# Norms of token blocks in one VectorE operation, a shared tile for the halves' last rows, and steps of two blocks in turn

## The chip, the cores and the metric

The kernel runs on one core of a Trainium2 chip. The engines are TensorE (PE in the profile, its weight loads PEld), VectorE (DVE), ScalarE (ACT), GpSimd (POOL) and SyncE (SP, which here only issues DMAs). Each engine takes its instructions in a fixed order and waits on semaphores. The metric is the device time of one execution in microseconds (us); lower is better.

## The reference

Two layers of a decoder run over 1040 prompt rows (16 learned rows and 1024 tokens) and 32 sample rows of width 1024. The change touches the first layer, a gated convolution; the attention layer behind it (`mla_query`, `attend`) stays as it is.

```python
def conv_mixer(h, prev, w_in, conv_w, w_out):
    L = h.shape[1]
    b_gate, c_gate, u, z = jnp.split(h @ w_in, 4, axis=-1)
    v = c_gate * u
    vc = jnp.concatenate([prev.astype(v.dtype), v], axis=1)
    y = conv_w[0] * vc[:, 0:L]
    for k in range(1, CONV_WIDTH):
        y = y + conv_w[k] * vc[:, k:k + L]
    out = (b_gate * y * jax.nn.silu(z)) @ w_out
    return out, vc[:, L:]
...
h = rmsnorm(x, pre_norm_g[l])
m, st = conv_mixer(h, conv_prev[l], w_in_conv[l], conv_w[l], w_out_conv[l])
x = x + rmsnorm(m, post_norm_g[l])
```

## The kernel before

All 1072 rows are treated as one matrix. Float32 operands are split into a high part (`hi_of`, an ACT copy with rounding) and a low part (`lo_of`, a subtraction, on DVE unless another engine is named), and a product takes three matmuls: high by high, high by low, low by high. The input product of the convolution is computed by a seven-product scheme for 2x2 blocks: the rows are cut into two halves of HT = 536 (`l` = 0 and 1), the width into two halves of 512. The seven left operands are held turned (features on partitions) in `H`: "11" and "21" are the first row half, "22" the second row half's upper width, "t1" to "t4" sums. The right operands of a pair of weight tiles are made by `weight_sums`: four POOL additions s1 to s4, then a high and a low part for each of seven operands.

**The opening.** Each half is read in five blocks (`PAIRS`): four of 128 rows and one of 24. `loaded` fetches a block, `normed` norms it: ACT squares it with a row sum (`junk`, `ss`), POOL makes the scale (`ta`, `qa`). A first-half block is then multiplied by the gain on POOL (`x<-x,gain`) and scaled on ACT (`x<-x,qa`); a second-half block takes one DVE operation (`x<-x,qa,gain`) and a subtraction `t3`. A block becomes steps in the list `todo`: `turn_in` (four PE transposes into a PSUM bank), for some steps `add_in` (two matmuls that add a finished part with +1 or -1), and `put` (a high part by ACT, a low part by DVE, both read from PSUM). A first-half block has two steps, a second-half block five: `chain` (t3), `plain` (22), `more` (t2), `other` (t1), `more` (t4). The two `more` steps add to the bank that `chain` filled, so each waits until the low part before it has been read. `Pair.start(ch)` computes two products of a unit early from the first half alone, for the columns of `CUTS[ch]` (256, then 280): 12 matmuls, an ACT copy `k1`, 12 more into the same bank, a copy `c11`. `Pair.multiply(n, ch)` is one of the seven products, 12 matmuls; the first unit runs `ORDER` = 1, 6, 5, 7, 3, 2, 4 (1 and 2 are the early ones) for `ch` 0 between the steps, then for `ch` 1. Fifteen more units follow.

**The end of the convolution.** Seven of eight gated rows go through DRAM (`gd`) into `g`, the last is written by four DVE operations (`Row.gate`). Then each pair of output weights is loaded (`raw`, three buffers) and split into `woh` and `wol`; `gated(b)` splits a token block of `g` into `gh` and `gl`, and PE computes `po`. The space of `woh` and `wol` is that of the input weights (`wr`), which is released when the last unit is done (`l2.close()`).

The order on each engine comes from the code's order and `tc.issue_after` (it keeps PE's instructions behind a marked one), through a scheduler that orders instructions by modelled times and gives tiles their slots. `tile(..., tag, bufs)` gives one of `bufs` slots, whose last reader must be done.

## Time and profile before

| | before |
|---|---|
| median of 3 runs | 1384.45 us (1381.78 to 1392.17) |
| profiled execution, its time | 1382.27 us |
| its span, first to last instruction | 1380.2 us |
| PE busy | 1295.8 us (94%) |
| DVE, ACT, POOL busy | 854.0, 680.1, 616.7 us |
| mean granted TensorE clock | 0.970 of full speed |

The span is cut into instructions by engine. A row of the timeline has a start, a length, the engine and line, what it writes and reads, the shape and a count; in brackets stands the idle time before it and the instruction that ended it. Matmuls overlap, so the distance of two starts tells more than a length. A share of busy time is a mean over stages: PE is almost always busy after the opening, so what an engine does beside it costs nothing there.

### The profile page before, as it was taken

What the parts mean: (1) busy time and instruction counts of PE and PEld (TensorE: products, weight loads), DVE (VectorE), ACT (ScalarE), POOL (GpSimd) and SP (SyncE); (2) the same over time, 40 slices, a digit from 0 to 9 for tenths busy, and PEclk for the clock granted to TensorE, in tenths of its full rate; (3) what the DMA queues carried; (4) which work ended last, traced back from release to release, by engine and by line L of the source; (5) the groups of instructions that cost most, each with busy time, mean ns of one, the idle gap of its engine ahead of it and who ended that gap; (6) DMA issues with size and microseconds to landing.
All of it is one profiled execution on the core that took longest, in us unless ns stands there. A gap on an engine that the chain in (4) does not pass through costs nothing.

```text
span 1380.2 us, 22927 instructions
## 1 busy us (share of the span) xinstructions
PE 1295.8 (94%) x8142; PEld 1169.0 (85%) x8142; DVE 854.0 (62%) x1750; ACT 680.1 (49%) x1401; POOL 616.7 (45%) x829
## 2 busy tenths in 40 slices
...
GB/s 173 47 64 52 75 79 50 76 62 48 80 247 92 90 85 106 47 147 208 212 80 1 40 62 25 47 63 25 62 41 32 72 215 176 113 148 129 114 168 169
DMA packets 107149, 131.86 MB, mean 96 GB/s; under 512 B 21135, under 2 KB 80187, under 8 KB 107035
## 3 DMA queue, kind: packets, MB, share of 16 engines
...
q8 instruction: 65, 1.06, 0.3%
...
## 4 chain that ended last, share of the span: by engine, by line
PE 42%; DMA 8%; DVE 5%; ACT 2%; issue 2%; POOL 1%; SPq 1%; DVEq 0%; POOLq 0%; ACTq 0%
PE pa L69 10%; PE ps L69 8%; PE pm L69 6%; PE pz L69 6%; PE pf L69 3%; DMA qh<-qd32h 3%; PE pr L69 3%; PE po L69 2%; DMA cn<-in_cache_ckv_dram,crow 2%; PE pc L1388 1%; PE pt L69 1%; DMA qd32h<-qxh 1%; DMA rr<-rl 1%; DVE big L850 1%; SPq L988 1%
## 5 line engine op out<-in xcount | busy, mean ns | idle before, releaser
L79 DVE TENSOR_TENSOR wl<-raw,wh 128x512 fp32r<-128x512 f32 x88 | 75.1, 857 | 99.3 <-ACT wh L74 95.9
L74 ACT ACTIVATE wh<-raw 128x512 fp32r<-128x512 f32 x88 | 55.1, 630 | 129.7 <-PE pa L69 48.2
L1169 ACT ACTIVATE p<-ps 128x512 f32<-128x512 f32 (+1 forms) x192 | 93.2, 492 | 38.3 <-PE ps L69 33.9
L74 ACT ACTIVATE ph<-p 128x512 fp32r<-128x512 f32 (+1 forms) x192 | 97.3, 527 | 22.1 <-POOL p L1174 20.7
L69 PE MATMUL pz<-ph,v 128*128 128x512 f32 (+3 forms) x384 | 104.8, 360 | 0.4 <-ACT ph L74 0.2
L79 POOL TENSOR_TENSOR nl<-cn,nh 128x256 fp32r<-128x256 f32 x64 | 62.0, 987 | 90.6 <-ACT nh L74 81.9
L79 POOL TENSOR_TENSOR pl<-p,ph 128x512 fp32r<-128x512 f32 (+2 forms) x75 | 82.5, 1109 | 32.7 <-ACT ph L74 26.1
L79 DVE TENSOR_TENSOR pl<-p,ph 128x512 fp32r<-128x512 f32 (+3 forms) x117 | 79.3, 684 | 26.7 <-ACT ph L74 26.2
L1025 DVE TENSOR_REDUCE mx<-pm 128x1 f32<-128x16 f32 (+6 forms) x210 | 83.6, 423 | 16.9 <-PE pm L69 16.4
L1174 POOL TENSOR_SCALAR_AFFINE_SELECT p<-p 128x127 f32<-128x127 f32 (+1 forms) x128 | 47.0, 370 | 81.2 <-ACT p L1169 61.6
L69 PEld LDWEIGHTS pz<-ph,v 128*128 128x128 f32 x384 | 66.3, 193 | 7.3 <-ACT ph L74 1.2
L69 PE MATMUL pm<-kh,qh 128*128 128x144 f32 (+6 forms) x210 | 61.6, 343 | 10.6 <-DMA qh<-qd32h 10.4
L69 PE MATMUL ps<-qh,kh 97*128 97x512 f32 (+3 forms) x192 | 68.6, 357 | 1.9 <-DMA qh<-mr 0.9
L69 PE MATMUL pz<-pl,v 128*128 128x512 f32 (+1 forms) x192 | 68.0, 355 | 1.6 <-DVE pl L79 1.2
L69 PE MATMUL ps<-qh,kl 97*128 97x512 f32 (+3 forms) x192 | 67.4, 351 | 0.0
L69 PE MATMUL ps<-ql,kh 97*128 97x512 f32 (+3 forms) x192 | 67.2, 350 | 0.0
L108 POOL TENSOR_SCALAR ta<-ss 128x1 f32<-128x1 f32 (+2 forms) x37 | 8.4, 227 | 126.6 <-ACT xa L605 52.7
L69 PE MATMUL pa<-x1h,wh 128*128 128x352 f32 x288 | 64.1, 329 | 0.0
L69 PE MATMUL pa<-x1h,wl 128*128 128x352 f32 x288 | 63.9, 328 | 0.0
L69 PE MATMUL pa<-x1l,wh 128*128 128x352 f32 x288 | 62.8, 326 | 0.0
L74 ACT ACTIVATE wh<-s 128x512 fp32r<-128x512 f32 x48 | 30.0, 630 | 64.8 <-POOL s L173 26.2
L79 DVE TENSOR_TENSOR wl<-s,wh 128x512 fp32r<-128x512 f32 x48 | 47.3, 989 | 21.3 <-ACT wh L74 20.0
...
## 6 DMA issues: line engine op xcount, KB each, us to landing
...
```

The costliest lines, as they stand in the source:

```text
L69: return pe.matmul(out, a, b, start=start, stop=stop, **kw)
L74: return act.activation(out, src, AF.Copy, scale=scale)
L79: (eng or dve).tensor_tensor(out, src, f(hi), ALU.subtract)
L108: pool.tensor_scalar(t[:r], ss[:r], 1.0 / n, EPS, ALU.mult, ALU.add)
L850: dve.tensor_tensor(qo, qo, sw, ALU.add)
L988: sp.dma_start(f(q[e * DN:e * DN + DN]), f(dn[h * DN:(h + 1) * DN]))
L1025: dve.tensor_reduce(mx[:, b, c:c + 1], pm[:, :off], AX.X, ALU.max)
L1169: act.activation(pt[:r, :n], ps[:r, :n], AF.Exp, scale=SCALE)
L1174: marks[h] = marks.get(h, []) + [pool.affine_select(pt[:r, :dn], pt[:r, :dn], [[1, dn]], ALU.is_ge, 0.0, base=META + c0 - t * P, channel_m ...
L1388: state["turned"] = pe.transpose(pc[:, r], cn[:, r, c * P:(c + 1) * P], ident)
```

## The change

Six edits are made together. (1) A block's gain and scale are one DVE operation for both halves. (2) The 24 last rows of the two halves share one tile: the first half's at partition 0, the second's at 32, 56 partitions in all with a POOL `memset` of the gap; one norm serves both, and this block comes fifth instead of fifth and tenth. (3) x tiles have four slots instead of three, and loads are issued in another order. (4) Steps of two second-half blocks are interleaved, `other` comes before the first `more`, and the early products, the weight sums and the banks (`spaces`) are placed anew. (5) The low parts of the first unit's five further weights are made on POOL (`eng=pool`). (6) `H["11"]` is allocated last in `hp`; the tiles `x1h`, `x1l` of the next stage are allocated first on the right side, and behind them the first two pairs of output weights (`wo2`), in the space of `H["11"]`.

```diff
-        H = {q: [hp.tile([P, HK, HT], F32R, name=f"h{q}{n}") for n in "hl"] for q in ("11", "21", "22", "t3", "t4")}
+        H = {q: [hp.tile([P, HK, HT], F32R, name=f"h{q}{n}") for n in "hl"] for q in ("21", "22", "t3", "t4", "11")}
...
-        def parts_w(src):
+        def parts_w(src, eng=None):
...
-            lo_of(wl, src, wh)
+            lo_of(wl, src, wh, eng)
...
-        def weight_sums(w1, w2, have=()):
+        def weight_sums(w1, w2, have=(), eng=None):
...
-            return {n: parts_w(src) for n, src in zip(ORDER, (a11, s2, s1, s3, s4, a12, a22)) if n not in have}
+            return {n: parts_w(src, eng) for n, src in zip(ORDER, (a11, s2, s1, s3, s4, a12, a22)) if n not in have}
...
         minus = xs.tile([P, P], F32R, name="minus")
         marks = {}
+
+        blocks = [(0, p) for p in range(4)] + [(None, 4)] + [(1, p) for p in range(4)]
+        ROWS = {0: 0, 1: 32}
+
         def loaded(l, p):
             lo, r = PAIRS[p]
-            x = xs.tile([P, D], F32, tag="x", bufs=3, name="x")
-            load_x(x, l * HT + lo, r, sp)
+            x = xs.tile([P, D], F32, tag="x", bufs=4, name="x")
+            if l is None:
+                pool.memset(x[:ROWS[1] + r], 0.0)
+                for l, at in ROWS.items():
+                    load_x(x[at:at + r], l * HT + lo, r, sp)
+            else:
+                load_x(x, l * HT + lo, r, sp)
             return x
         def normed(l, p, x):
-            lo, r = PAIRS[p]
+            r = PAIRS[p][1] if l is not None else ROWS[1] + PAIRS[p][1]
             junk = wr.tile([P, D], BF16, tag="sm", bufs=3, name="junk")
             ss = stat.tile([P, 1], F32, tag="ss", name="ss")
             act.activation(junk[:r], x[:r], AF.Square, accum_out=ss[:r])
             rs = rstd_of(ss, D, r, "a")
+            dve.scalar_tensor_tensor(x[:r], x[:r], rs[:r], gain[:r], ALU.mult, ALU.mult)
             if l == 0:
-                pool.tensor_tensor(x[:r], x[:r], gain[:r], ALU.mult)
-                act.activation(x[:r], x[:r], AF.Copy, scale=rs[:r])
-                return x
-            dve.scalar_tensor_tensor(x[:r], x[:r], rs[:r], gain[:r], ALU.mult, ALU.mult)
+                return first_half(p, x, slice(0, r))
+            rows = slice(0, r) if l else slice(ROWS[1], r)
             t3 = wr.tile([P, 512], F32, tag="sm", bufs=3, name="t3")
-            dve.tensor_tensor(t3[:r], x[:r, :512], x[:r, 512:], ALU.subtract)
-            return x, t3
+            dve.tensor_tensor(t3[rows], x[rows, :512], x[rows, 512:], ALU.subtract)
+            return ([] if l else first_half(p, x, slice(0, PAIRS[p][1]))) + second_half(p, x, t3, rows)
         def put(p, q, pt):
             lo, r = PAIRS[p]
             hi_of(hi, pt[:, :, :r])
             lo_of(lo_, pt[:, :, :r], hi)
-        def turn_in(p, pt, src):
+        def turn_in(p, pt, src, rows):
             r = PAIRS[p][1]
             for k in range(HK):
-                marks["pe"] = pe.matmul(pt[:, k, :r], src[:r, k * P:(k + 1) * P], ident[:r, :r], start=k == 0, stop=k == HK - 1, is_transpose=True, skip_group_check=True).ins
+                marks["pe"] = pe.matmul(pt[:, k, :r], src[rows, k * P:(k + 1) * P], ident[rows, rows], start=k == 0, stop=k == HK - 1, is_transpose=True, skip_group_check=True).ins
         def add_in(p, pt, sign, q):
             tag = spaces.pop(0)
             return four(turned() if tag == "t" else bank(tag))
-        def first_half(p, h):
...
+        def first_half(p, h, rows):
...
+        def second_half(p, h, t3, rows):
...
-                turn_in(p, at[0], t3)
...
-            return [chain, plain, lambda: more("t2", minus, "11"), other, lambda: more("t4", plus, "21")]
+            return [chain, plain, other, lambda: more("t2", minus, "11"), lambda: more("t4", plus, "21")]
...
         keep_warm(turned(), WARM)
         hi_of(plus, ident)
         hi_of(minus, ident, -1.0)
-        blocks = [(l, p) for l in range(2) for p in range(5)]
-        xt = {b: loaded(*b) for b in blocks[:2]}
+        xt = {blocks[0]: loaded(*blocks[0])}
         sp.dma_start(gain, i["pre_norm_g"][0:1].to_broadcast((P, D)))
+        xt[blocks[1]] = loaded(*blocks[1])
+        w0 = conv_w(0)
         xt[blocks[2]] = loaded(*blocks[2])
-        w0 = conv_w(0)
         z0 = conv_w(2)
+        xt[blocks[3]] = loaded(*blocks[3])
         w1 = conv_w(1)
-        todo = []
-
-        def stage(*some):
-            for b in some:
-                h = normed(*b, xt.pop(b))
-                todo.extend(first_half(b[1], h) if b[0] == 0 else second_half(b[1], *h))
-                n = blocks.index(b) + 3
-                if n < len(blocks):
-                    xt[blocks[n]] = loaded(*blocks[n])
-
-        stage(*blocks[:2])
-        a0, a1, b0, b1 = w0[:, :512], w0[:, 512:], z0[:, :512], z0[:, 512:]
-        first = Pair(None, 0, {1: parts_w(a0), 2: parts_w(a1)}, early=True)
-        second = Pair(None, 1, {1: parts_w(b0), 2: parts_w(b1)}, early=True)
-        spaces += ["t", "t", "c0", "c1"] * 8
+
+        def stage(n):
+            res = normed(*blocks[n], xt.pop(blocks[n]))
+            if n + 4 < len(blocks):
+                xt[blocks[n + 4]] = loaded(*blocks[n + 4])
+            return res
+
+        first = Pair(None, 0, {1: parts_w(w0[:, :512]), 2: parts_w(w0[:, 512:])}, early=True)
+        spaces += ["t", "t", "c0", "c1", "a1", "b1"]
+        todo = stage(0) + stage(1)
         steps(todo, 4)
-        stage(*blocks[2:5])
-        for unit in (first, second):
-            for _ in unit.start(0):
-                steps(todo, 2 if len(todo) > 3 else 1)
+        second = Pair(None, 1, {1: parts_w(z0[:, :512]), 2: parts_w(z0[:, 512:])}, early=True)
+        spaces += ["t", "t", "c0", "c1"] * 3
+        todo = stage(2) + stage(3)
+        early = [x for unit in (first, second) for x in (unit.start(0), unit.start(1))]
+        for n in (0, 0, 2, 2):
+            next(early[n])
+            steps(todo, 1)
+        todo += stage(4)
+        first.w.update(weight_sums(w0, w1, have=(1, 2), eng=pool))
+        first.sums()
+        steps(todo, 2)
+        spaces[:] = ["t", "c0", "t", "c1", "a0", "b0"] * 2
+
+        todo2 = [stage(n) for n in (5, 6)]
+        todo += todo2[0][:3] + todo2[1][:1] + todo2[0][3:4] + todo2[1][1:3] + todo2[0][4:] + todo2[1][3:]
+        next(early[1])
+        steps(todo, 3)
+        next(early[1])
+        steps(todo, 4)
+        next(early[3])
+        steps(todo, 4)
+        next(early[3])
         steps(todo, len(todo))
-        first.w.update(weight_sums(w0, w1, have=(1, 2)))
-        first.sums()
-        stage(*blocks[5:7])
-        del spaces[6:]
-        for unit in (first, second):
-            for _ in unit.start(1):
-                steps(todo, 3)
-        spaces += ["t", "c1", "a1", "t", "b1", "a0"] * 4
-
-        stage(*blocks[7:])
+        spaces[:] = ["t", "c1", "t", "a1", "b1", "a0"]
+        todo2 = [stage(n) for n in (7, 8)]
+        todo = todo2[0][:3] + todo2[1][:1] + todo2[0][3:4] + todo2[1][1:3] + todo2[0][4:] + todo2[1][3:]
+
         for n in ORDER:
             if n not in (1, 2):
                 with tc.issue_after(marks["pe"]):
                     first.multiply(n, 0)
-                steps(todo, 3)
+                steps(todo, 3 if n in (6, 5) else 2)
+        steps(todo, len(todo))
...
         l2.close()
         l0.close()
+        x1s = ctx.enter_context(ExitStack())
+        x1p = x1s.enter_context(sbuf("x1p", side="right"))
+        x1h = x1p.tile([P, NK, T], F32R, name="x1h")
+        x1l = x1p.tile([P, NK, T], F32R, name="x1l")
+
+        w2 = l1.enter_context(sbuf("wo2", side="right"))
         wr = l1.enter_context(sbuf("wo"))
...
         wo = []
         for k in range(NK):
             raw = load_w(i["w_out_conv"][0, k * P:(k + 1) * P])
-            wh, wl = (wr.tile([P, D], F32R, name=f"wo{n}{k}") for n in "hl")
+            wh, wl = ((w2 if k < 2 else wr).tile([P, D], F32R, name=f"wo{n}{k}") for n in "hl")
             hi_of(wh, raw)
             lo_of(wl, raw, wh)
             wo.append((wh, wl))
...
-        x1s = ctx.enter_context(ExitStack())
-        x1p = x1s.enter_context(sbuf("x1p", side="right"))
-        x1h = x1p.tile([P, NK, T], F32R, name="x1h")
-        x1l = x1p.tile([P, NK, T], F32R, name="x1l")
```

ACT at the start, before (`junk` is the square, `x<-x,qa` the scaling, `wh` a weight's high part, `pt` and `c` PSUM banks):

```order
L198 ACTIVATE junk,ss<-x 128x1024 x3
L202 ACTIVATE x<-x,qa 128x1024
L74 ACTIVATE wh<-raw 128x512 x4
L202 ACTIVATE x<-x,qa 128x1024
L74 ACTIVATE h11h<-pt 128x4x128
```

ACT at the start, now:

```order
L207 ACTIVATE junk,ss<-x 128x1024 x2
L74 ACTIVATE wh<-raw 128x512 x2
L74 ACTIVATE h11h<-pt 128x4x128
L74 ACTIVATE h21h<-pt 128x4x128
L207 ACTIVATE junk,ss<-x 128x1024
L74 ACTIVATE wh<-raw 128x512
L74 ACTIVATE h11h<-c_204 128x4x128
L74 ACTIVATE wh<-raw 128x512
```

The scalings are gone, and the first block is read from PSUM behind two squares and two weight parts instead of three, four and two scalings.

POOL behind the first squares, before (`s_355` to `s_357` are s1, s2, s4; `raw<-raw` is s3):

```order
L172 TENSOR_TENSOR s_355<-raw 128x512
L108 TENSOR_SCALAR ta<-ss 128x1
L201 TENSOR_TENSOR x<-x,gain 128x1024
L173 TENSOR_TENSOR s_356<-raw,s_355 128x512
L174 TENSOR_TENSOR raw<-raw 128x512
L110 TENSOR_TENSOR qa<-ta,mhalf 128x1
L108 TENSOR_SCALAR ta<-ss 24x1
L201 TENSOR_TENSOR x<-x,gain 24x1024
L175 TENSOR_TENSOR s_357<-raw,s_356 128x512
```

POOL in the same place, now:

```order
L110 TENSOR_TENSOR qa<-ta,mhalf 56x1
L172 TENSOR_TENSOR s_343<-raw 128x512
L173 TENSOR_TENSOR s_344<-raw,s_343 128x512
L174 TENSOR_TENSOR raw<-raw 128x512
L79 TENSOR_TENSOR wl<-s_344,wh 128x512
L79 TENSOR_TENSOR wl<-s_343,wh 128x512
L79 TENSOR_TENSOR wl<-raw,wh 128x512
L175 TENSOR_TENSOR s_345<-raw,s_344 128x512
L79 TENSOR_TENSOR wl<-s_345,wh 128x512
L108 TENSOR_SCALAR ta<-ss 128x1
```

The gain products have left the queue; four low parts now stand between the scale of the shared block and that of the first full block of the second half (the last `ta`).

DVE at the end of the convolution, before (`g` is the gate's output):

```order
L346 SCALAR_TENSOR_TENSOR g<-k_4343,s 128x280
L79 TENSOR_TENSOR gl<-g,gh 128x896
L79 TENSOR_TENSOR gl<-g,gh 128x128
L79 TENSOR_TENSOR gl<-g,gh 128x1024
L79 TENSOR_TENSOR wol_4581<-raw,woh_4580 128x1024
```

DVE at the end of the convolution, now:

```order
L354 SCALAR_TENSOR_TENSOR g<-k_4330,s 128x280
L79 TENSOR_TENSOR wol_4576<-raw,woh_4575 128x1024
L79 TENSOR_TENSOR wol_4582<-raw,woh_4581 128x1024
L79 TENSOR_TENSOR wol_4588<-raw,woh_4587 128x1024
L79 TENSOR_TENSOR gl<-g,gh 128x896
L79 TENSOR_TENSOR gl<-g,gh 128x128
```

Three low parts of output weights have moved ahead of the token blocks' low parts; on ACT their high parts have moved ahead of `gh` in the same way.

## Rows read from the trace of the kernel before

**Rows 1.** Windows; columns: stretch, busy time by engine, granted clock, DMA share, GB/s.

```profile
0.00:50.00 50.00, 30.76 (x179) 27.74 (x180) 26.29 (x32) 32.39 (x60) 26.41 (x34) 0.80 0.51 149
10.00:20.00 10.00, 4.77 (x19) 3.75 (x19) 6.99 (x7) 8.70 (x14) 8.61 (x6) 0.50 0.65 174
...
100.00:150.00 50.00, 50.00 (x407) 49.96 (x406) 33.46 (x52) 18.05 (x37) 30.28 (x31) 1.00 0.26 78
```

**Rows 2.** Timeline of PE, the opening up to the first transposes of the constants.

```profile
12.04 1.97 PE L218 MATMUL pt<-ident,x 128*128 128x128 f32 x8 [6.09 <-ACT x L202]
...
19.89 0.58 PE L69 MATMUL a<-h11l,wh 128*128 128x256 f32 x1
...
20.48 0.41 PE L69 MATMUL a<-h11h,wh 128*128 128x256 f32 x1
20.70 0.41 PE L69 MATMUL a<-h11l,wh 128*128 128x256 f32 x1
...
23.98 0.28 PE L69 MATMUL b<-h11h,wh 128*128 128x256 f32 x1
24.10 0.28 PE L69 MATMUL b<-h11l,wh 128*128 128x256 f32 x1
...
49.81 1.09 PE L218 MATMUL c<-ident,x 128*128 128x128 f32 x4 [3.50 <-DVE ht4l L79]
...
54.13 0.39 PE L69 MATMUL b<-sums,wh 128*128 128x256 f32 x2
...
85.66 0.25 PE L499 MATMUL pt<-ident,rows 44*128 44x44 f32 x1
```

**Rows 3.** Timeline of ACT, the opening.

```profile
5.18 1.06 ACT L198 ACTIVATE junk<-x 128x1024 bf16<-128x1024 f32 x1 [2.49 <-DMA x<-in_x_prompt_dram]
...
9.78 1.06 ACT L198 ACTIVATE junk<-x 128x1024 bf16<-128x1024 f32 x1 [2.30 <-DMA x<-in_x_prompt_dram]
...
10.84 1.15 ACT L202 ACTIVATE x<-x,qa 128x1024 f32<-128x1024 f32 x1
...
13.38 1.15 ACT L74 ACTIVATE wh<-raw 128x512 fp32r<-128x512 f32 x2 [0.35 <-DMA raw<-in_w_in_conv_dram]
```

**Rows 4.** Timeline of POOL, the opening.

```profile
6.69 0.56 POOL L110 TENSOR_TENSOR qa<-ta,mhalf 128x1 f32<-128x1 f32 x1
...
8.46 4.67 POOL L201 TENSOR_TENSOR x<-x,gain 128x1024 f32<-128x1024 f32 x2
...
22.84 1.26 POOL L173 TENSOR_TENSOR s<-raw,s 128x512 f32<-128x512 f32 x1
...
28.88 1.71 POOL L175 TENSOR_TENSOR s<-raw,s 128x512 f32<-128x512 f32 x1
```

**Rows 5.** Timeline of DVE, the opening.

```profile
12.54 5.10 DVE L79 TENSOR_TENSOR wl<-raw,wh 128x512 fp32r<-128x512 f32 x4 [12.54 <-ACT wh L74]
...
32.43 1.28 DVE L204 SCALAR_TENSOR_TENSOR x<-x,qa,gain 128x1024 f32<-128x1024 f32 x1 [0.45 <-POOL qa L110]
...
37.34 0.69 DVE L79 TENSOR_TENSOR wl<-raw,wh 128x512 fp32r<-128x512 f32 x1 [0.69 <-ACT wh L74]
...
48.98 0.68 DVE L79 TENSOR_TENSOR ht4l<-c,ht4h 128x512 fp32r<-128x512 f32 x1
49.58 0.68 DVE L79 TENSOR_TENSOR ht3l<-pt,ht3h 128x512 fp32r<-128x512 f32 x1
```

**Rows 6.** Timelines of PE, ACT and DVE at the end of the convolution.

```profile
394.07 2.07 PE L69 MATMUL po<-woh,gh 128*128 128x512 f32 x4 [4.22 <-ACT woh L74]
...
398.50 0.77 PE L69 MATMUL po<-wol,gh 128*128 128x512 f32 x2
...
392.98 2.93 ACT L74 ACTIVATE woh<-raw 128x1024 fp32r<-128x1024 f32 x3
...
390.44 0.45 DVE L346 SCALAR_TENSOR_TENSOR g<-k,s 128x280 f32<-128x280 f32 x1
...
394.31 3.49 DVE L79 TENSOR_TENSOR wol<-raw,woh 128x1024 fp32r<-128x1024 f32 x3
```

8 lines of the change are left out of this document (4 added, 4 removed).

## The prediction

> **What bounds the kernel now.** First read the windows [rows 1]. From 100 us on PE is busy in every microsecond at the full granted clock, so what DVE, ACT and POOL do there costs nothing. In the first 50 us PE is busy for 30.76, at a mean clock of 0.80, and between 10 and 20 us for 4.77 at 0.50, the lower of its two levels (1.2 of 2.4 GHz). So the opening is a place where time can be had; the other that this change touches is the start of the output product. Then follow PE through the opening [rows 2]: it waits 6.09 us for the first normed block, and later 3.50 for a low part. Three marks serve for comparison: the first product runs on from 19.89 (it needs a low part there), the first sum product of `multiply` (n = 6) starts at 54.13, and the transposes of the constants (L499) at 85.66. In both programs PE has the same work behind it at this last mark, and its order from there to the output product is the same; PE is full there, so whatever this mark gains or loses reaches the output product undiminished. The sum is made against the profiled execution, 1382.27 us, which lies 2.2 below the median of the runs.
>
> **The change part by part.** Call the blocks b0 to b8 in the new order; b4 is the shared one, b5 to b8 the full ones of the second half. I walk along each engine's new queue with durations of rows, 0.05 us for a hand-over.
>
> *Loads and first norms.* The half-megabyte loads were used first at 5.18 (first), 9.78 (fourth) and 13.38 (sixth) [rows 3], 1.8 us apart once they run. In the new order that puts b0 at 5.2, the gain at 6.7, b1 at 8.3, w0 at 9.8, b2 at 11.6, z0 at 13.4, b3 at 15.2, w1 at 17 and the small b4 at 17.4. b0: the square ends at 6.24 and the scale at 7.25 [rows 3, 4], the DVE operation takes 1.28 [rows 5], so the transposes start at 8.6 instead of 12.04. What went were POOL's 4.67 us for two gain products [rows 4] and ACT's 1.15 for a scaling [rows 3]. b1: square from 8.3, scale at 10.3, DVE until 11.6, transposes (1.97 us [rows 2]) until 13.6. ACT then has w0's high parts until 10.9 (1.15 for two [rows 3]), b0's two, the square of b2, z0's first part and b1's first at 14.4. DVE, after b1, makes w0's and b0's low parts, z0's, norms b2, and comes to b1's first low part at 15.9 to 16.5. The product runs on from 16.5 instead of 19.89: **3.4 us earlier**.
>
> *First half.* PE's 11 matmuls left of the first product go at the low clock, 0.22 apart; the clock then came back at about 23.98, 4.1 us after the steady start, with 0.12 [rows 2]. I take the same delay, so 20.6. The 48 early matmuls of `ch` 0, eight transposes of b2 and b3 and b4's two small steps end at 26.1; b4's low part is read at 26.9, and `ch` 1 runs on from there.
>
> *POOL's new work.* b4's scale is ready at 19.5. Then s1 to s3 at 1.26 [rows 4], three low parts taken at 1.3 (the nearest row, an addition of the same shape) and s4: until 28.6. ACT's high part of s4 waits for that, and behind it on ACT stand the square of b5 (29.2 to 30.3), one high part, and the copy `k1` at 31.2, which PE's second half of `ch` 1 waits for; PE gets there at 30.8, so this queue just sets the pace. POOL then does one more low part and b5's scale (31.4); DVE norms b5 until 32.8. PE needs b5 only at 34.5. SP: the load of w3 now waits for s4 too (28.6), with b8's load behind it; b8 lands at about 32 and is squared at 40.4, so this costs nothing while s4 is less than 8 us late.
>
> *Second half.* From here DVE is the bound: between the norm of b6, which ends at 35.3, and the last low part that PE waits for stand two norms (2.4), three subtractions and nine full low parts (0.60 from start to start [rows 5], 7.2) and a small one (0.2): 9.8 us, and 1.2 of waiting while ACT squares b7. That ends at 46.4; PE has waited 3.3 and 2.4 us for it, and its two last matmuls let n = 6 start at 47.0. Two of POOL's additions for the second unit lie beside the norm of b8; four low parts beside POOL's products took 5.10 where one alone takes 0.69 [rows 5], so I add 0.8: 47.8 instead of 54.13. Up to L499 PE has 7 products of 256 columns (12 x 0.118 = 1.42 each, 9.9), 5 of 280 (1.55, 7.8), six groups of transposes (0.5 each, half of what the row at the low clock gives, 3.0) and six additions of two 512-column matmuls (0.47, 2.8): 23.5. After waits of this size the clock fell before (the four transposes at 49.81 took 1.09 [rows 2]); I add one episode like the first, 4.1 us at half, 2.1. L499 then starts at 73.4 instead of 85.66: **-12.3 us**. The lead grows from 6.3 to 12.3 because the old program still had waits and b4's second half to go after its 54.13.
>
> *Output weights.* PE waits 4.22 us, until 394.07, and runs at the low clock until 398.50 [rows 6]. In the new order ACT makes two high parts before 389.5, the third until about 390.9 (1.0 each [rows 6]; it waits for the unit's last weights), `gh` until 391.9: PE can start at 392.0. But DVE's low parts still stand behind the last gate, which ends at 390.89: three at 1.2 until 394.5, then `gl` at 395.6, and PE's ninth matmul needs `gl`. So PE has done 8 matmuls by 395.6 where it had done 3 or 4, and has waited twice. If the clock stays low for 4.4 us after that, the gain is 0.25; if it is high, 2.5. I take **-1.0**, nearer the low end, since the old wait of 4.22 was followed by the low clock. The loads of later output weights start 3.4 us earlier (the first `wol` ends at 392.1 instead of 395.5), and I find no PE wait for them.
>
> *Without cost.* The new place of `H["11"]` and of `x1h` moves no instruction. The fourth x slot only removes waits. b4's shared norm saves a square, a scale and a norm (about 1 us each of ACT, POOL and DVE, off the path). POOL's `memset` lies between two scales at 10.6, with 2 us to spare. Later queues show a few swapped neighbours (the turns in the output stage, the sample attention); no row prices them; I take 0, within 1 either way.
>
> **Sum.** 1382.27 - 12.3 - 1.0 = **1369.0**.
>
> **A rule against this change.** Four low parts on DVE took 5.10 beside POOL's gain products [rows 5], and s4 at 28.88 took 1.71 where s2 took 1.26 [rows 4]. The Trainium skill (Perfetto Trace Analysis, "Optimizing Scalar/DVE Operations") says that moving work between these two engines might not help, because they share a read port, and SBUF — State Buffer ("Who interferes with whom") says that one of the two then blocks for the whole instruction of the other. By that rule the low parts on POOL cost what they save on DVE; the time would be that of the second rival.
>
> **Rivals.** *More is gained.* PE's waits in the second half don't lower the clock (2.1), POOL's additions don't meet b8's norm (0.8), the output product finds the high clock (1.5 more): 1369.0 - 4.4 = 1364.6. Against it speaks the low clock behind each long wait before. *POOL gives part back.* Its nine operations on the weight sums take 1.71 instead of 1.28 each, 3.9 us; 0.4 of it PE doesn't see, the rest delays ACT's high part of s4, hence the copy `k1` and the square of b5, one for one: +3.5, and the output stage at its low end 0.8: 1373.3. For it: POOL's row of 1.71; against it: most of DVE's work in that stretch reads PSUM, and s2 beside such work took 1.26. *The clock doesn't come back.* Work in pieces with a wait every few us could leave PE at 1.2 GHz through the opening. From 20.6 to 47.8 it has some 20.5 us of work at the full clock, so 20.5 more, of which 5.7 lie in its waits: +14.8, which is 1384, no gain; if it also holds through half of the 23.5 us behind n = 6, +11.8: 1396, slower. It decides from the point where less than a third of the opening runs at the full clock. Against it: 0.80 as a mean of the old opening, which had longer waits. *The output weights aren't early at all* (DVE's order undoes it): 1369.8, inside the forecast's own range.
>
> **How the numbers follow.** Forecast (1366 to 1372) 0.53; more gained (1362 to 1366) 0.17; POOL gives back (1372 to 1378) 0.20; the clock stays low, or something that the walk doesn't see (above 1378) 0.10, of which 0.04 above 1398. A measurement of this kernel can tell about 1% from no change: against the median of 1384.45 that is 1370.6. The forecast's range lies about two thirds below it: 0.53 x 0.6 + 0.17 = 0.49 for faster; 0.04 for slower; 0.47 for the same. The range leaves out the last case and the ends of two: 1363 to 1377.
>
> **What would show it.** Right: PE's first transposes at about 8.6, the steady start near 16.5, n = 6 near 47.8, L499 near 73, then PE full until about 377.5, `po` starting about 2 us after the last matmul of the units. DVE without a pause between 36 and 46. Wrong: POOL's operations on the weight parts near 1.7 and ACT waiting for s4 beyond 30 (second rival); a granted clock near 0.5 between 25 and 45 (third); or a gain at L499 that is gone by 400, which would mean that the units were not bound by PE alone.

## The result and the profile after

The changed kernel takes 1371.64 us (median of 6 runs, 1369.06 to 1373.01), the kernel before 1386.74 on the same chip (6 runs): ratio 0.9887, 95% interval 0.986 to 0.9914. Measured a second time, it takes 1370.41 (6 runs) against 1385.17 (12 runs): 0.9895, 0.9872 to 0.9918. It is 1.1% faster. The profiled execution takes 1369.06 with a span of 1367.3, where before it was 1382.27 and 1380.2.

First the windows of the changed kernel; the columns are the stretch, the busy time of PE, PEld, DVE, ACT and POOL, the granted clock, the DMA share and GB/s.

```profile
0.00:50.00 50.00, 34.02 (x209) 29.81 (x210) 32.69 (x42) 29.27 (x63) 25.60 (x37) 0.83 0.52 151
...
10.00:20.00 10.00, 5.93 (x25) 5.23 (x26) 8.57 (x11) 7.79 (x15) 3.93 (x9) 0.50 0.88 247
...
40.00:50.00 10.00, 3.20 (x15) 1.87 (x14) 9.57 (x12) 4.85 (x10) 5.09 (x5) 0.84 0.00 1
...
380.00:390.00 10.00, 6.84 (x29) 4.90 (x28) 7.61 (x9) 4.82 (x6) 0.00 (x0) 1.00 0.94 293
```

PE is busy for 34.02 us of the first 50 where it was 30.76 [rows 1], at a clock of 0.83. Between 40 and 50 it has work for 3.20 us only, while DVE is busy for 9.57. The output product, which begins between 380 and 390, finds the clock at 1.00.

PE in the opening (start, duration, engine, line, operation, and in brackets the wait before it with what ended it):

```profile
8.43 1.29 PE L226 MATMUL pt<-ident,x 128*128 128x128 f32 x8 [2.50 <-DVE x L209]
...
16.84 0.58 PE L69 MATMUL a<-h11l,wh 128*128 128x256 f32 x1 [1.41 <-DVE h11l L79]
...
29.27 0.40 PE L69 MATMUL a<-h11l,wh 128*128 128x280 f32 x1 [0.23 <-DVE h11l L79]
...
36.81 0.60 PE L226 MATMUL b<-ident,x 128*128 128x128 f32 x4
...
45.14 0.50 PE L69 MATMUL c<-h21h,plus 128*128 128x512 f32 x1 [3.03 <-DVE sums L79]
...
49.83 0.80 PE L69 MATMUL pt<-h21h,plus 128*128 128x512 f32 x1 [3.49 <-DVE sums L79]
...
50.85 0.63 PE L69 MATMUL b<-sums,wh 128*128 128x256 f32 x2
...
76.29 0.25 PE L516 MATMUL pt<-ident,rows 44*128 44x44 f32 x1
```

Against [rows 2]: the first transposes start at 8.43 (12.04), the first product runs on from 16.84 (19.89), its second columns run on from 29.27, b5's first transposes are at 36.81, the first sum product is at 50.85 (54.13), and the constants' transposes, the mark of the forecast, at 76.29 (85.66): **9.4 us earlier**, where 12.3 were forecast. In the second execution the mark is at 77.82. There the load of b4 landed later, its square started at 19.07 instead of 18.25, and the whole queue behind it moved with it: the first sum product came 0.81 later. (The first experiment below, whose opening is the same, has the square at 18.26 and the mark at 76.02.) So a mark compared from one execution each is good to some 1.5 us, and better where b4's square is compared too.

The queues behind that, POOL, DVE and ACT:

```profile
20.27 1.27 POOL L172 TENSOR_TENSOR s<-raw 128x512 f32<-128x512 f32 x1
...
21.62 2.15 POOL L173 TENSOR_TENSOR s<-raw,s 128x512 f32<-128x512 f32 x1
...
23.72 1.74 POOL L174 TENSOR_TENSOR raw<-raw 128x512 f32<-128x512 f32 x1
...
29.14 1.29 POOL L175 TENSOR_TENSOR s<-raw,s 128x512 f32<-128x512 f32 x1
...
20.33 2.29 DVE L209 SCALAR_TENSOR_TENSOR x<-x,qa,gain 56x1024 f32<-56x1024 f32 x1 [0.95 <-POOL qa L110]
...
22.66 1.65 DVE L214 TENSOR_TENSOR t<-x 24x512 f32<-24x512 f32 x1
...
33.40 2.31 DVE L209 SCALAR_TENSOR_TENSOR x<-x,qa,gain 128x1024 f32<-128x1024 f32 x1
...
36.73 1.27 DVE L209 SCALAR_TENSOR_TENSOR x<-x,qa,gain 128x1024 f32<-128x1024 f32 x1
...
45.60 1.90 DVE L209 SCALAR_TENSOR_TENSOR x<-x,qa,gain 128x1024 f32<-128x1024 f32 x1
...
49.10 0.68 DVE L79 TENSOR_TENSOR sums<-pt,sums 128x512 fp32r<-128x512 f32 x1
...
30.46 0.63 ACT L74 ACTIVATE wh<-s 128x512 fp32r<-128x512 f32 x1 [1.85 <-POOL s L175]
...
31.00 1.04 ACT L207 ACTIVATE junk<-x 128x1024 bf16<-128x1024 f32 x1
```

POOL's s2 and s3 take 2.15 and 1.74, where s2 took 1.26 before [rows 4], and s4 ends at 30.43; ACT waits for it and only then squares b5. DVE's norms of b4, b5 and b8 take 2.29, 2.31 and 1.90, where the row of before has 1.28 [rows 5]; POOL works beside each of them. The norm of b6 ends at 38.00.

The end of the convolution, PE and ACT:

```profile
380.18 0.29 PE L69 MATMUL b<-ht4h,wl 128*128 128x280 f32 x1
...
382.38 0.73 PE L69 MATMUL po<-woh,gh 128*128 128x512 f32 x2 [1.90 <-ACT gh L74]
...
385.98 0.73 PE L69 MATMUL po<-woh,gl 128*128 128x512 f32 x2 [1.25 <-DVE gl L79]
...
398.38 0.73 PE L69 MATMUL po<-wol,gh 128*128 128x512 f32 x2 [0.29 <-DVE wol L79]
...
387.94 1.06 ACT L74 ACTIVATE woh<-raw 128x1024 fp32r<-128x1024 f32 x1 [4.45 <-DMA raw<-in_w_out_conv_dram]
```

The last matmul of the units starts at 380.18 and the output product at 382.38, 2.2 us later; before, it was 389.56 and 394.07 [rows 6]:

```profile
389.56 0.29 PE L69 MATMUL b<-ht4h,wl 128*128 128x280 f32 x1
```

It then waits 1.25 for `gl` and, in short pieces (0.29 the longest), for weights: ACT splits them as their loads land.

Where the difference lies, by marks in PE's timeline: the constants' transposes; the units, to the start of their last matmul; from there to the first input product of the attention layer (`pa`, with the output product and the latent products); to the first transposes of the sample attention's cache (`pc`); to the product with `uv` (`pu`); to the last matmul. All kernels of the study, one execution each (the column "n = 6" is the start of the first sum product, which has that number):

| kernel | median us | ratio (95%) | n = 6 | mark | units | to `pa` | to `pc` | to `pu` | to end |
|---|---|---|---|---|---|---|---|---|---|
| before | 1386.74 | | 54.13 | 85.66 | 303.9 | 143.1 | 564.8 | 233.0 | 43.2 |
| after | 1371.64 | 0.9887 (0.986, 0.9914) | 50.85 | 76.29 | 303.9 | 140.7 | 568.1 | 228.5 | 43.2 |
| after, again | 1370.41 | 0.9895 (0.9872, 0.9918) | 51.66 | 77.82 | 303.9 | 141.2 | 564.7 | 232.1 | 43.2 |
| e1_weights_old | 1373.54 | 0.9911 (0.9888, 0.9934) | 50.83 | 76.02 | 303.9 | 142.4 | 567.0 | 236.5 | 43.2 |
| e2_low_dve | 1377.50 | 0.993 (0.9904, 0.9956) | 51.29 | 76.31 | 303.9 | 141.9 | 566.3 | 238.6 | 42.1 |
| e3_norms_late | 1370.78 | 0.9886 (0.9861, 0.9912) | 47.65 | 73.01 | 303.9 | 141.7 | 564.9 | 237.9 | 42.1 |
| the same, again | 1369.52 | 0.9897 (0.9873, 0.992) | 46.67 | 72.34 | 303.9 | 139.5 | 563.0 | 236.9 | 42.1 |
| e4_norm_only | 1377.62 | 0.9931 (0.9907, 0.9956) | 50.22 | 80.93 | 303.9 | 143.3 | 567.4 | 238.7 | 42.1 |
| e5_sums_wait | 1374.63 | 0.9925 (0.9903, 0.9946) | 53.61 | 79.28 | 304.3 | 141.4 | 562.8 | 232.1 | 42.0 |
| e6_no_interleave | 1368.89 | 0.988 (0.9848, 0.9913) | 51.93 | 79.21 | 303.9 | 139.2 | 566.0 | 230.3 | 42.1 |
| e7_sums_later | 1361.01 | 0.9835 (0.9808, 0.9862) | 49.62 | 74.68 | 303.9 | 140.1 | 561.5 | 227.9 | 43.0 |
| e8_chain | 1374.20 | 0.9914 (0.9881, 0.9948) | 54.59 | 81.05 | 303.9 | 139.7 | 566.6 | 231.6 | 43.2 |
| e9_both | 1377.49 | 0.9941 (0.9908, 0.9974) | 53.72 | 80.18 | 303.9 | 141.1 | 564.0 | 239.0 | 43.2 |
| e10_warm | 1369.94 | 0.9908 (0.9877, 0.9938) | 52.25 | 78.35 | 304.3 | 138.9 | 563.6 | 228.3 | 43.2 |

The units take 303.9 us in nearly every row: PE is full there, and what the mark gains reaches the output product undiminished, as the prediction said. But single stretches after `pa` differ by up to 11 us, and all of it by 16 (832.3 to 848.2), between kernels most of which were changed in their first 80 us only. For the opening I therefore read the mark; a median that differs from another by less than some 5 us says little about an edit of the opening.

The traces show what differs there: the granted clock. The stretch from `pc` to `pu` of the changed kernel and of the one with late norms:

```profile
1088.98:1317.45 228.47, 203.71 (x1135) 156.03 (x1136) 168.47 (x347) 173.63 (x348) 103.57 (x119) 0.94 0.51 153
```

```profile
1083.53:1321.44 237.91, 212.81 (x1140) 162.91 (x1141) 168.85 (x347) 174.89 (x350) 105.32 (x119) 0.91 0.48 147
```

PE is idle for 25 us in both; it is busy 9 us longer in the second, at 0.91 instead of 0.94. From `pa` to the end PE is idle for 45 to 51 us in all fourteen executions, and the time at the lower clock (twice the missing share of the mean clock, times the length) goes from 27 us where the stretch took 832.3 to 61 where it took 847.0 and 848.2; over the fourteen the two go together with a correlation of 0.92. Executions with the same order on PE lie close: 228.5 and 232.1 for the changed kernel's `pc` to `pu`, 237.9 and 236.9 for the late norms, 238.6 for the low parts on DVE, whose order on PE from `pa` to `pu` is that of the late norms. So the order that the scheduler chose for a later stretch goes with how long the clock is low in it; why is not shown.

### The profile page after: what moved, and what is told of

Same layout as the page of the kernel before. It is cut to its first block, busy times and chain, and to the rows that moved or that the text cites. A ratio compares the mean times of both kernels' runs of the same rounds, so it can differ in the third digit from the quotient of the medians.

```text
span 1367.3 us, 22924 instructions
## 1 busy us (share of the span) xinstructions
PE 1291.8 (94%) x8142; PEld 1163.4 (85%) x8142; DVE 854.9 (63%) x1749; ACT 673.8 (49%) x1394; POOL 609.3 (45%) x828
## 4 chain that ended last, share of the span: by engine, by line
PE 74%; DMA 10%; DVE 6%; ACT 3%; issue 3%; POOL 2%; SPq 1%; DVEq 0%; POOLq 0%; ACTq 0%
PE b L69 11%; PE pa L69 10%; PE po L69 8%; PE ps L69 8%; PE c L69 7%; PE a L69 6%; PE pm L69 6%; PE pz L69 6%; DMA qh<-qd32h 3%; PE pf L69 3%; PE pr L69 3%; PE pc L1406 2%; DMA cn<-in_cache_ckv_dram,crow 1%; PE pk L69 1%; PE pt L69 1%
## 5 line engine op out<-in xcount | busy, mean ns | idle before, releaser
L79 DVE TENSOR_TENSOR wl<-raw,wh 128x512 fp32r<-128x512 f32 x86 | 70.6, 823 | 85.4 <-ACT wh L74 82.2
L74 ACT ACTIVATE ph<-p 128x512 fp32r<-128x512 f32 (+1 forms) x192 | 97.5, 527 | 22.0 <-POOL p L1192 20.6
L79 DVE TENSOR_TENSOR wl<-s,wh 128x512 fp32r<-128x512 f32 x45 | 44.4, 989 | 20.5 <-ACT wh L74 18.8
```

Of the source, the lines that this page charges most:

```text
L74: return act.activation(out, src, AF.Copy, scale=scale)
L79: (eng or dve).tensor_tensor(out, src, f(hi), ALU.subtract)
```

## The experiments

**The output weights as before,** with the places of `x1h` and of `H["11"]` (all other edits stay).

```diff
-            wh, wl = ((w2 if k < 2 else wr).tile([P, D], F32R, name=f"wo{n}{k}") for n in "hl")
+            wh, wl = (wr.tile([P, D], F32R, name=f"wo{n}{k}") for n in "hl")
```

> The changed kernel with its output-weight edit undone: the first output weights and x1's halves stand where they stood before. The opening should be as in the changed kernel (constants' transposes at 76.3 within 0.5). Theory: the early weights are worth little, because the first output product then waits for the low part of the gate (1.25) and for the later weights' loads instead; from the last matmul of the units to the first latent matmul it took 107.2 us in the changed kernel and 107.6 before, so this run should show 107.6 and a time 0.4 to 0.9 above the changed kernel's: about 1372.3. Rival: the early weights are worth their head start of 2.3 us and the 2.2 us of low clock that went with it: 1376.1.

The mark is at 76.02. To the first latent product it takes 106.8 us, no more than the changed kernel's 107.2: up to there the early weights are worth nothing. But to `pa` it takes 142.4 instead of 140.7 and 141.2, and the median is 1.9 us above the changed kernel's first and 3.1 above its second. The difference arises in the latent stage. First this kernel's POOL and ACT, then the changed kernel's POOL:

```profile
512.90 1.90 POOL L782 TENSOR_TENSOR raw<-raw,cols 128x1024 f32<-128x1024 f32 x1 [4.35 <-DMA raw<-in_w_in_mla_dram]
...
514.83 1.15 ACT L74 ACTIVATE wh<-raw 128x512 fp32r<-128x512 f32 x2 [1.94 <-POOL raw L782]
```

```profile
511.45 1.90 POOL L784 TENSOR_TENSOR raw<-raw,cols 128x1024 f32<-128x1024 f32 x1 [2.39 <-issue]
```

POOL's scaling of the next weights starts 26.2 us after the first latent product (486.72) and waits for their DMA; in the changed kernel it starts 24.1 us after it (487.34), and ACT's high parts and DVE's low parts behind it are earlier by as much. Over all rows: from the first latent product to `pa` the three kernels without edit (6) (before, this one, the norm alone) took 35.3 to 35.6 us, the eleven other executions 33.3 to 34.2. The theory had 0.4 to 0.9 us and the rival some 4.5; up to `pa` it is 1.2 to 1.7, nearer to the theory, and in a place that neither named. The weights and the places of the other tiles were undone together, so which of them it is stays open.

**Norms of b7 and b8 behind b6's t2.** The edit is an order on DVE, with no operation more or less; a few pieces on ACT and one addition on POOL change places with it, and PE's order up to the mark is the same.

```diff
+            with ExitStack() as late:
+                if l == 1 and p > 1:
+                    late.enter_context(tc.issue_after(marks["t2"]))
-            dve.scalar_tensor_tensor(x[:r], x[:r], rs[:r], gain[:r], ALU.mult, ALU.mult)
+                dve.scalar_tensor_tensor(x[:r], x[:r], rs[:r], gain[:r], ALU.mult, ALU.mult)
```

> The changed kernel, but the norms of b7 and b8 stand on VectorE behind the low part of b6's t2, on which the first sum product waits. The amount of work is the same on every engine. Theory (VectorE's order sets the first sum product, not its amount of work): two norms (1.27 and 1.90) and two subtractions (0.68 and 1.15) leave the stretch from 40.8 to 49.8, so the first sum product starts at about 46.6 instead of 50.85, PE has the other products of the first columns (some 7 us) while VectorE makes the norms, and the constants' transposes start at about 72.5 instead of 76.3: 1367.9. Rival (VectorE is bound through the whole second half, by its amount): what is gained at the first sum product is waited for again before b7's and b8's steps, the constants' transposes stay within 1 us of 76.3, and the time at 1371.6.

DVE and PE of this kernel:

```profile
45.90 0.68 DVE L79 TENSOR_TENSOR sums<-pt,sums 128x512 fp32r<-128x512 f32 x1
...
46.49 1.28 DVE L212 SCALAR_TENSOR_TENSOR x<-x,qa,gain 128x1024 f32<-128x1024 f32 x1
...
46.63 0.79 PE L69 MATMUL pt<-h21h,plus 128*128 128x512 f32 x1 [1.55 <-DVE sums L79]
...
47.65 0.63 PE L69 MATMUL b<-sums,wh 128*128 128x256 f32 x2
```

The low part that PE waits for starts at 45.90 (49.10 in the changed kernel), b7's norm comes behind it, the first sum product starts 3.2 us earlier and the mark lies at 73.01, 3.3 earlier. The theory holds: the order on DVE and not its amount of work set this stretch. In the total it does not show: 1370.78 against 1371.64, since `pc` to `pu` took 237.9, at the lower clock shown above. Run once more beside the changed kernel:

> The kernel with the norms of b7 and b8 behind b6's t2 once more, beside the changed kernel on the same chip. The opening should show the same 73.0 (3.3 us earlier than the changed kernel). Theory: that much reaches the end but for what the order of the sample attention gives or takes: 1 to 4 us below the changed kernel. Rival: the later order takes it all: no difference.

The mark is at 72.34, 5.5 before that of the changed kernel measured beside it (0.8 of which is b4's load, which landed earlier), and the median 1369.52 against 1370.41: 0.9 less, with intervals that overlap widely. The theory for the opening holds again. From `pa` to the end it took 842.0 us against 840.0, and 844.9 against 839.7 in the first pair, so the later order takes part of the gain; how much the total keeps these runs can't resolve.

**The norm alone**, in the kernel before.

```diff
             if l == 0:
-                pool.tensor_tensor(x[:r], x[:r], gain[:r], ALU.mult)
-                act.activation(x[:r], x[:r], AF.Copy, scale=rs[:r])
+                dve.scalar_tensor_tensor(x[:r], x[:r], rs[:r], gain[:r], ALU.mult, ALU.mult)
                 return x
```

> The kernel before with one edit alone: the first half's blocks are normed by one VectorE operation, too; loads, order, sums and small blocks as before. Theory: the first transposes start 3.4 us earlier (8.6), the steady start of the first product moves from 19.9 to about 17, and the rest of the old opening follows undiminished: the constants' transposes at 82.6 instead of 85.7 and the time 3 us below the kernel before, 1383.7. So about a third of the changed kernel's 9.4 us would be this edit's. Rival 1: five norms of 1.28 in front of low parts on VectorE, and the old queue behind, give the gain back: constants' transposes at 85.7, 1386.7. Rival 2: nearly all of the gain is this edit's: at 77, 1378.

The steady start is at 16.17, 3.7 us earlier, and the mark at 80.93, 4.7 earlier. That is half of the changed kernel's 9.4: more than the theory's third, and neither rival. The median, 1377.62, is 7.5 us below that of the kernel before, measured beside it (1385.09); it lies at the second rival's 1378, but the mark that this rival needed (77) did not come.

**POOL's sums wait for b4's norm.**

```diff
+            if l is None:
+                marks["go"] = pool.tensor_copy(stat.tile([P, 1], F32, name="go")[rows], t3[rows, :1]).ins
...
-        first.w.update(weight_sums(w0, w1, have=(1, 2), eng=pool))
+        with tc.issue_after(marks["go"]):
+            first.w.update(weight_sums(w0, w1, have=(1, 2), eng=pool))
```

> The changed kernel, but GpSimd's sums of the first weights wait for the end of b4's norm and subtraction on VectorE (a copy of 24 numbers of its result stands ahead of them). Theory (the two engines held each other up, and that delayed b4's low part and the second columns of the first product): b4's norm takes 1.28 and not 2.29, the subtraction 0.6 and not 1.65, PE's first low part of that stretch starts at 22.3 and not 24.34, the second columns run on from 27.2 and not 29.27, and the constants' transposes start at 74.3 to 75.3: 1369.6 to 1370.6. Rival (the chain of GpSimd's sums, ScalarE's high part of s4 and the square of b5 sets the pace): the sums end 0.9 us later than before, so do b5's norm and all that follows, and the constants' transposes start at 76.3 to 77.2: 1371.6 to 1372.5.

Its DVE, the norm and the subtraction of b4 with POOL idle:

```profile
21.32 1.28 DVE L209 SCALAR_TENSOR_TENSOR x<-x,qa,gain 56x1024 f32<-56x1024 f32 x1 [1.74 <-POOL qa L110]
...
22.63 0.68 DVE L214 TENSOR_TENSOR t<-x 24x512 f32<-24x512 f32 x1
```

1.28 and 0.68 instead of 2.29 and 1.65, as expected; POOL's s2 and s3 take 1.29 and 1.26. Yet the second columns run on from 29.95, no earlier than 29.27, and the mark goes to 79.28: the rival, and more than it said. Part of that is b4's load, which landed 1.0 us later than in the changed kernel's first execution (square at 19.24) and 0.2 later than in its second, whose mark is 1.5 earlier. With that allowed for, the second columns gain 0.3 us of the 2.1 forecast: b4's lengthened norm was nearly covered. The sums, which now end 2.1 us later, 1.0 of it by the load, were not. How much of the 1.5 to 3.0 at the mark is theirs stays open, because PE's clock was low between 30 and 40 (0.66) and b6's square, behind a copy of PE's product, came at 37.04 instead of 33.98.

**The low parts on DVE.**

```diff
-        first.w.update(weight_sums(w0, w1, have=(1, 2), eng=pool))
+        first.w.update(weight_sums(w0, w1, have=(1, 2)))
```

> The changed kernel, but the five low parts of the first weight sums are made by VectorE, as before, and not by GpSimd; the four sums stay on GpSimd at the same place. Theory (GpSimd's queue of nine operations, with s4 at its end and ScalarE's high part of s4 and b5's square behind it, sets the second half; VectorE has 9 of 13 us free between 25 and 36): s4 ends about 4 us earlier (26.2 instead of 30.4), b5's norm moves forward with it, five low parts of 0.6 fit into VectorE's pauses, the first sum product starts at about 48 instead of 50.85 and the constants' transposes at 73.5 instead of 76.3: 1369. Rival (VectorE is what bounds the second half, so every microsecond put on it counts): 3 us more on VectorE, constants' transposes at 78 to 79: 1374.

Neither: the mark is at 76.31, where it was in the changed kernel's first execution and 1.5 before its second; b4's square started at 18.19, as in the first. s4 ends at 28.19 and b6's norm at 35.46, 2.5 us earlier; but PE's second columns run on 2.1 us later (31.32, after a wait of 2.35 for ACT's high part of b4), and on DVE both later norms still stand ahead of b6's t2. From b6's norm to the first sum product it took 15.8 us instead of 12.85, with 2.7 of pauses on DVE: what was won ahead of that norm was lost behind it. Three microseconds of work moved between the two engines, and at the mark no difference can be told.

**No interleaving.**

```diff
-        todo += todo2[0][:3] + todo2[1][:1] + todo2[0][3:4] + todo2[1][1:3] + todo2[0][4:] + todo2[1][3:]
+        todo += todo2[0] + todo2[1]
```

(and the same for b7 and b8)

> The changed kernel, but the steps of b5 and b6, and of b7 and b8, stand one block after the other instead of interleaved. Theory (a block's steps depend on each other by way of ScalarE and VectorE, and the other block's steps fill PE's waits): the first sum product starts 2 us later (53) and the constants' transposes 2 to 3 us later (79): 1374. Rival (VectorE's queue sets the stretch whatever PE's order): both within 1 us of the changed kernel's 50.85 and 76.3: 1371.6.

The first sum product starts at 51.93, the mark lies at 79.21: 2.9 and 1.4 us after the changed kernel's two. With b4's load allowed for (square at 18.95) the first sum product is 0.4 later and the mark 1.5 to 2.2. That is the theory's direction, at the mark nearly its size. The median, 1368.89, lies 2.8 and 1.5 below the changed kernel's all the same: the stretch to `pa` took 139.2 and that to `pu` 230.3. Here the mark and the total speak against each other most plainly.

**POOL's queue reordered: the sums first, the scale of b5 ahead.**

```diff
-        first.w.update(weight_sums(w0, w1, have=(1, 2), eng=pool))
+        s1 = wr.tile([P, 512], F32, tag="sm", bufs=3, name="s1")
+        pool.tensor_tensor(s1, a21, a22, ALU.add)
+        pool.tensor_tensor(a21, a21, a11, ALU.subtract)
+        pool.tensor_tensor(a11, a11, s1, ALU.subtract)
+        pool.tensor_tensor(a12, a12, a11, ALU.add)
...
+        todo2 = [stage(5)]
+        first.w[5] = parts_w(s1, pool)
+        todo2.append(stage(6))
+        first.w[6] = parts_w(a11, pool)
```

> The changed kernel with GpSimd's queue reordered: the four sums first, three of them in place, the scale of b5 ahead of all low parts but one, ScalarE's high part of s4 behind b5's square. Work and engines are as in the changed kernel. Theory (the chain of sums, s4's high part, squares and norms of b5 and b6 sets the start of the second half): b6's norm ends at about 34.5 instead of 38.0, the first sum product starts 2.5 to 3 us earlier (48) and the constants' transposes at 73.5: 1369. Rival (VectorE's order of norms and low parts behind that sets it, the start of the second half is covered): constants' transposes within 1 us of 76.3: 1371.6.

A miss: the mark is at 81.05, 4.8 us after the changed kernel's first and 3.2 after its second. DVE and PE show why:

```profile
27.30 2.29 DVE L209 SCALAR_TENSOR_TENSOR x<-x,qa,gain 128x1024 f32<-128x1024 f32 x1 [1.07 <-POOL qa L110]
...
31.78 0.24 DVE L79 TENSOR_TENSOR h11l<-c,h11h 128x96 fp32r<-128x96 f32 x1
...
32.07 0.60 PE L69 MATMUL a<-h11l,wh 128*128 128x280 f32 x1 [2.67 <-DVE h11l L79]
```

b5's norm did come early, and took 2.29 beside POOL's additions, its subtraction 1.64; on DVE both stand ahead of b4's low part (31.78), for which PE waits 2.67 before the second columns. Both reorderings together:

> The changed kernel with both reorderings: GpSimd's queue (sums first, b5's scale ahead of the low parts) and VectorE's (norms of b7 and b8 behind the low part of b6's t2). Theory (two waits one behind the other, so the gains add): first sum product at about 45 instead of 50.85, constants' transposes at 70.5 to 71 instead of 76.3 (3.3 from VectorE's order, as measured, and 2 to 2.8 from GpSimd's): 1366 to 1367. Rival (one covers the other): constants' transposes at 73, the time 1370 to 1371 as with VectorE's order alone.

80.18 and 1377.49: the same trouble at the second columns (33.33), and a mark only 0.9 before that of GpSimd's order alone. b4's load landed 1.25 later here (squares at 19.28 and 18.03), so that some 2.1 of VectorE's 3.3 us may be in it. Theory and rival both fall all the same: their marks were 70.5 to 73.

**More junk transposes,** to hold the clock.

```diff
-        keep_warm(turned(), WARM)
+        keep_warm(turned(), WARM + 12)
...
+            for q in range(8):
+                marks["pe"] = pe.transpose(junk[:, q % 4], ident, ident).ins
```

(eight behind b0's transposes, four behind b1's)

> The changed kernel with 24 more junk transposes on PE: 12 before the first block's, 8 between the first and the second block's, 4 behind the second's, all in stretches in which PE waits. They are there to hold the granted clock at 1.00 between 10 and 23 us, where it was 0.50. Theory (GpSimd's sums and ScalarE's queue set the pace up to b5's norm, PE's clock is covered): clock 1.00 there, more waits of PE between 20 and 30, constants' transposes within 1 us of 76.3. Rival (PE's half clock counts): some 9 us of busy time at half clock go, constants' transposes at 72 to 73, and 3 to 4 us less in all.

```profile
10.00:20.00 10.00, 7.14 (x56) 6.31 (x55) 8.57 (x11) 8.20 (x17) 4.45 (x8) 1.00 0.88 252
```

```profile
26.15 0.60 PE L69 MATMUL a<-h11l,wh 128*128 128x280 f32 x1 [1.53 <-DVE h11l L79]
...
42.41 0.86 PE L226 MATMUL pt<-ident,t 128*128 128x128 f32 x4 [4.10 <-DVE t L214]
```

The clock was 1.00, the second columns ran on from 26.15 instead of 29.27, and the mark is at 78.35 all the same: PE waits 4.10 at 42.41 for b6's t3. No gain, as the theory had it, though 2 us beyond its range, and other queues changed too. Nor is it shown that the transposes held the clock: between 10 and 20 us it was 1.00 in four executions without them too (late norms again, sums that wait, sums later, both reorderings). The cleaner case is the kernel with the late norms, whose two executions have the same instructions in the same order and a different clock. The first, then the second:

```profile
10.00:20.00 10.00, 6.21 (x27) 5.11 (x26) 8.48 (x11) 7.46 (x15) 3.46 (x7) 0.50 0.90 247
...
40.00:50.00 10.00, 6.91 (x32) 5.34 (x32) 8.37 (x13) 5.98 (x13) 3.79 (x5) 0.83 0.01 2
```

```profile
10.00:20.00 10.00, 6.43 (x28) 5.44 (x27) 8.63 (x11) 7.76 (x15) 3.56 (x8) 1.00 0.89 247
...
40.00:50.00 10.00, 6.93 (x44) 5.40 (x42) 8.89 (x12) 6.55 (x13) 4.05 (x5) 1.00 0.01 2
```

At 0.50 and 0.83 the mark was at 73.01, at 1.00 in both at 72.34, 0.7 earlier. But most of this is b4's load; its square, again the first and then the second:

```profile
18.81 1.06 ACT L207 ACTIVATE junk<-x 56x1024 bf16<-56x1024 f32 x1 [2.10 <-DMA x<-in_x_sample_dram]
```

```profile
18.27 1.06 ACT L207 ACTIVATE junk<-x 56x1024 bf16<-56x1024 f32 x1 [1.68 <-DMA x<-in_x_sample_dram]
```

That is 0.54, and b6's norm ends 0.53 earlier (38.02 instead of 38.55). For the half clock 0.1 us is left at the mark, and 0.45 at the first sum product.

**The sums later,** behind the norms of b5 and b6.

```diff
-        first.w.update(weight_sums(w0, w1, have=(1, 2), eng=pool))
-        first.sums()
...
         todo2 = [stage(n) for n in (5, 6)]
+        first.w.update(weight_sums(w0, w1, have=(1, 2), eng=pool))
+        first.sums()
```

> The changed kernel, but GpSimd's sums of the first weights and their parts are written behind the norms of b5 and b6, so that they start at about 33 instead of 20.3; the squares of b5 and b6 no longer stand behind ScalarE's high part of s4. Theory (as the run with GpSimd's queue reordered showed, an early norm of b5 stands on VectorE ahead of low parts that PE waits for; and the sums' parts now come late for the first sum product): constants' transposes at 79 to 81. Rival (the sums' early place is what delayed b5's norm, with nothing gained for it): b6's norm ends 3 us earlier, constants' transposes at 73 to 74.

```profile
23.72 1.27 DVE L209 SCALAR_TENSOR_TENSOR x<-x,qa,gain 128x1024 f32<-128x1024 f32 x1
...
29.60 1.28 DVE L209 SCALAR_TENSOR_TENSOR x<-x,qa,gain 128x1024 f32<-128x1024 f32 x1 [0.52 <-POOL qa L110]
...
37.07 1.15 ACT L74 ACTIVATE wh<-s 128x512 fp32r<-128x512 f32 x2 [0.72 <-POOL s L173]
...
48.59 0.80 PE L69 MATMUL pt<-h21h,plus 128*128 128x512 f32 x1 [2.35 <-DVE sums L79]
```

The theory fell. b5's norm starts at 23.72, alone and so in 1.27, and b6's at 29.60, 7 us before the changed kernel's; the low parts that PE's second columns need are not held up (28.15). Of these 7 us only 1.2 reach the first sum product, because the sums now stand in the second half and ACT's and DVE's parts wait for them. The mark is at 74.68, 1.6 and 3.1 us before the changed kernel's. In the total this is the best kernel of the study: 1361.01 (4 runs, 1359.42 to 1363.60), ratio 0.9835 (0.9808 to 0.9862), 9.4 us below the changed kernel measured beside it. The opening explains a third of that at most; most of the rest lies behind `pa`, where it was quickest (561.5 and 227.9, with 27 us at the lower clock where the changed kernel had 44).

**The changed kernel again.**

> The changed kernel once more, unaltered. From the first transposes of the sample attention (pc) to the product with the up weights (pu) it took 228.5 us in its first profile, 233.0 in the kernel before and 230 to 239 in the experiments so far, whose instructions in that stretch stand in other orders on the engines. Theory (the order decides): 228 to 230 again, and a median within 2 us of 1371.6. Rival (it varies from execution to execution): anything between 228 and 239 for the same program, and then no difference of a few us in the total may be put down to an edit. Constants' transposes at 76.3 within 0.5, whichever holds.

Neither as it stands: `pc` to `pu` took 232.1 with the same instructions, outside the theory's 228 to 230, but the rival's width of 11 us is not that of one program: 237.9 and 236.9 for the kernel with late norms, 238.6 for another with its order. From `pa` to the end it was 839.7 and 840.0, and the median is within 2 us, as the theory said. The mark was off by 1.5 us: 0.8 by b4's load, the rest behind the first sum product, where the clock was lower (0.71 instead of 0.82 between 50 and 60 us).

## Why the prediction was right

The forecast was 13.3 us below the profiled execution of before; it came out at 13.2, and at 11.0 in the second profiled execution (medians: 15.1 and 14.8 below those of before). By its own steps:

- **Loads and first norms: right.** Transposes at 8.43 (8.6 forecast), running on at 16.84 (16.5). The run with the norm alone shows this edit as half of what the mark gains. Of the other half the interleaving has 1.5 to 2.2 us; the shared tile, the fourth x slot and the order of loads had no run of their own.
- **First half: 2.3 us too early, without cost.** The second columns ran on from 29.27, not 26.9, partly since the clock came back at about 23 and not at 20.6. The run with the high clock brought them to 26.15 and gained nothing, and in the two executions with the late norms the clock is worth 0.1 us at the mark.
- **POOL's new work: the term that was mis-sized.** s4 ended at 30.43 (28.6 forecast) and b5's norm at 35.71 (32.8). 0.8 of it is a later load of b4; the rest is that POOL's s2 and s3 took 1.4 us more than their 1.26 each, and DVE's norm of b5 1.0 more. Against it stand some 0.3 that the low parts saved: POOL's followed each other at 1.25, and I had taken 1.3 and a hand-over. I had priced contention at 0.8, beside b8's norm alone. b5's norm is 2.9 late and so is the mark. With the order of this kernel the one follows the other: where b4 came 0.82 later (the second execution), b5's norm came 0.80 and the first sum product 0.81 later. In another order it need not: the mark stayed where b6's norm came 2.5 earlier (low parts on DVE) and moved by 1.6 to 3.1 where it came 7 earlier (sums later). The rows fit a turn-taking: b4's norm (20.33 to 22.62) ends 1.08 behind s1's end (21.54), s2 (to 23.77) 1.15 behind the norm's, the subtraction (to 24.31) 0.54 behind s2's, and s3 (to 25.46) 1.15 behind the subtraction's: each takes about its own time once the other is done. That agrees with the Trainium skill (SBUF — State Buffer, "Who interferes with whom"), by which the ports that the two share are an exclusive lock and the order of issue decides who blocks; low parts that DVE reads from PSUM were not lengthened.
- **Second half: right in size, but only for this order.** From the end of b6's norm to the first sum product I had 12.5 us and it was 12.85, with one pause of 0.71 on DVE; from there to the mark I had 25.6 and it was 25.44. But "DVE is the bound" holds for what stood in its queue, not for its amount of work: with the same work in another order it was 9.1 (38.55 to 47.65), and with three microseconds more for DVE the mark did not move by more than two executions differ. What set it, and what I had counted without asking whether it must stand there, was that two norms and two subtractions which nobody needed yet stood ahead of the low part that PE waited for.
- **Output weights: the size right, by another way.** From the units' last matmul to the first latent product the changed kernel gained 0.4 us (107.6 to 107.2), and to `pa` 2.4 and 2.0; -1.0 was forecast. Without edit (6) 1.2 to 1.7 of that go, in the latent stage. The clock stayed high, against the forecast, and in its place PE waited for `gl` and for the loads of later weights, of which I had said that I found no wait (0.29 is the longest that a row marks).
- **Without cost: right, as a sum.** From `pa` to the end 840.9 became 839.7 and 840.0. That it came within the 1 us of the forecast is luck: other orders of the same work took 832.3 to 848.2 there.

So the mechanism held for most of the walk, but that the total was hit to 0.1 us is luck, by errors of opposite sign: 2.9 too much gain forecast at the mark, 1.4 too little from there to `pa` and 1.2 too little behind it. **The rivals:** that more is gained did not happen. That POOL gives part back happened, with some 2.1 (the 2.9 less 0.8 for b4's load) instead of the 3.5 of its price, and with the sign that I had named for it, ACT waiting for s4 beyond 30; the median, 1371.64, lies just under the 1372 at which that rival began. The clock came back, and where it was low up to the first sum product it cost 0.1 at the mark, because PE did not set the pace there; the rival's price had counted PE's work as if it did. The output weights were early. The low parts were worth about the same on either engine (76.31 at the mark, against 76.29 and 77.82). By that, the rule of the Trainium skill (Perfetto Trace Analysis, "Optimizing Scalar/DVE Operations") that moving work between the two might not help agrees with the runs for this edit, in its outcome; that the shared port is the reason is not shown. The norm, which left POOL altogether, made half of the gain at the mark.

What stays open is why the clock is low for longer behind `pa` in some of these kernels. The same program varied there by up to 3.6 us in one stretch (by 0.3 and 2.9 over all three), and PE's order in the sample attention differs between most of these kernels as they are built. Most of the 9 us by which the kernel with the later sums leads go with the clock there; whether its order or chance gave it that clock was not tried, since it has one trace.
